# Eight orders of the high-part and low-part matmuls in layer 1 of a two-layer backbone

## The chip, the core and the metric

The kernel runs on one NeuronCore of a Trainium2 chip. The engines that matter here are TensorE (PE in the profile, with its weight loads as a row of their own, PEld), VectorE (DVE), ScalarE (ACT) and SyncE (SP), which issues the DMAs. The metric is the time of one execution on the device in microseconds. The kernel as it stands takes 1834.39 us, the median of three runs (1833.95 to 1835.42).

## The reference

Two layers act on 256 tokens of width 2048. Layer 0 (retention and Fourier mixing, with a context of 256 more tokens) is not touched by the table of orders. Layer 1 is the short gated convolution:

```python
def _odd_layer(h, w_in, conv_w, w_out, rows):
    bg, cg, xt, g = jnp.split(h @ w_in, 4, axis=-1)
    y = bg * _conv3(cg * xt, conv_w, rows) * jax.nn.silu(g)
    return y @ w_out
...
    x = x + gate_x * yx
...
return _rmsnorm(x, final_norm_w)
```

`h` is the modulated norm of `x` (256 by 2048), `w_in` is 2048 by 16384, `w_out` is 4096 by 2048. All of it is float32.

## The kernel before, in words

Every activation lies channel-major: channels on the 128 partitions, the 256 tokens on the free axis. A product in float32 is carried by three passes of a faster format: each operand is split exactly into a high and a low part of 12 bits (x = hi + lo), and hi·hi + lo·hi + hi·lo is summed in PSUM. An activation tile holds its two parts side by side, 512 columns: high in 0 to 255, low in 256 to 511.

The weights stream in as tiles of 128 by 2048 (1 MB, `load_raw`, issued by SP, three buffers). Each tile is cut into quarters of 512 columns (`split_w`): ScalarE casts a quarter to its high part `whi` (line 95), VectorE subtracts to get the low part `wlo` (line 59). There are six buffers of each, so ScalarE and VectorE work ahead of TensorE by up to six quarters, and then wait until a matmul frees one.

`group_t` (line 119) makes 256 output columns. It runs over weight tiles (`kt`), their quarters (`pc`), and in a quarter over four blocks of 128 by 128 weights: two k-chunks (`k2`) by two halves of the output columns (`m`). For each block there are two matmuls. The one with the high part of the weights streams all 512 columns of the activation (high and low part), so it makes hi·hi in the left half of a PSUM bank and hi·lo in the right half. The one with the low part of the weights streams only the 256 columns of the high activations into the left half. In what follows H is a matmul of the first kind (128x512 in the profile) and L one of the second kind (128x256). Each matmul has a weight load of its own, also where two in a row use the same weights. `lr` (line 178) later adds the two halves.

`group_t` serves layer 0 (for the keys with two streams at once, `hx` and `hc`), the output projection of layer 0 (`w0o`), layer 1 and its output projection (`w1o`). In layer 1 the loop over `b` (line 700) calls it four times for each of 16 blocks, 64 groups of two weight tiles in all: 64 x 2 x 4 x 4 = 2048 H and 2048 L, on the input tiles `h1_0` to `h1_7` (`h` in the profile). The output projection then runs over the tiles `y1` (`y`): seven blocks by `group_t` (448 H and 448 L) and the eighth by `group_d`, whose matmuls are all of 256 columns, three in a row for each block of weights: high by high, high by low, low by high. `group_n` (`gN`) is a form with 512 columns throughout.

A scheduler that simulates the program sets the order on each engine. It keeps the order in which `group_t` issues its matmuls, except where an operand would be late: there it pulls matmuls of the next group in between. At the start of layer 1, where the tiles `h1` are still being made (lines 196 to 198), the first two groups are interleaved in this way.

Of the kernel before, what the change touches and what calls it, by code (L numbers as in the profile page):

```python
"""Two-layer hybrid retention / Fourier / short-convolution backbone with a context prefix.

Everything runs in channel-major form (channels on partitions, tokens on the free axis), so
modulation, gates, norms' weights and the convolution are per-partition scalars, and no
activation is ever transposed.  Matrix products are carried by float32r passes: each operand is
split exactly into two 12-bit parts (x = hi + lo) and hi*hi + lo*hi + hi*lo is accumulated in PSUM.
"""
# [13 lines left out]
D = 2048  # L21
T = 256
H = 8
DK = 128
P = 128
EPS = 1e-6

# columns of the packed per-channel vectors
C_C, C_CC, C_AB0, C_NW0, C_ABG, C_NW1, C_FNW, C_LOG, C_CV, C_SEL = 0, 16, 32, 64, 80, 144, 160, 176, 192, 288
N_COLS = 290  # L30
# columns of the packed shape-only tables
# [4 lines left out]
def body(tc, a, out):  # L36
    nc = tc.nc
    es = ExitStack()
    with es:
# [27 lines left out]
        # ---------------------------------------------------------------- constants  # L67
# [11 lines left out]
        # ---------------------------------------------------------------- weight stream  # L79
# [5 lines left out]
        def split_w(raw, spare=None):  # L85
            """Exact 12-bit parts of a weight tile, by quarters; the last quarter can use spare slots."""
            parts = []
            for pc in range(4):
                sl = raw[:, pc * 512:(pc + 1) * 512]
                if spare and pc == 3:  # L90
                    hi, lo = spare()
                else:
                    hi = wp.tile([P, 512], F32R, tag="whi", bufs=6, name="whi")
                    lo = wp.tile([P, 512], F32R, tag="wlo", bufs=6, name="wlo")
                nc.scalar.copy(hi[:], sl)  # L95
                sub(lo[:], sl, hi[:])
                parts.append((hi, lo))
            return parts
# [6 lines left out]
        def bg():  # L105
            """One background task at every second weight tile."""
            if quiet[0]:
                return
            turn[0] ^= 1
            if tasks and turn[0]:  # L110
                tasks.pop(0)()
# [7 lines left out]
        def group_t(wd, i0, nkt, streams):  # L119
            """Channel-major product of 256 output columns; per stream a pair of banks [hi.W + lo.hi | lo.W]."""  # L120
            ps = [psum("gT") for _ in streams]
            for kt in range(nkt):
                raw = load_raw(wd[i0 + kt])
                bg()
                for pc, (hi, lo) in enumerate(split_w(raw)):
                    for k2 in range(2):
                        kc = kt * 8 + pc * 2 + k2
                        fst, lst = kc == 0, kc == nkt * 8 - 1
                        for t, st in zip(ps, streams):
                            x = st[kc // 2]  # L130
                            for m in range(2):
                                c0 = k2 * 256 + m * 128
                                mm(t[:, m, :], hi[:, c0:c0 + 128], x[:, kc % 2, :], fst, False)
                                mm(t[:, m, 0:256], lo[:, c0:c0 + 128], x[:, kc % 2, 0:256], False, lst)
                    if pc % 2:
                        hook()
            return ps

        def group_d(wd, i0, nkt, x):
            """As group_t for one stream, with all three products summed in place: a bank of two column halves."""  # L140
            t = bank("gD")
            for kt in range(nkt):
                raw = load_raw(wd[i0 + kt])
                bg()
                for pc, (hi, lo) in enumerate(split_w(raw)):
                    for k2 in range(2):
                        kc = kt * 8 + pc * 2 + k2
                        xh, xl = x[kc // 2][:, kc % 2, 0:256], x[kc // 2][:, kc % 2, 256:512]
                        for m in range(2):
                            c0 = k2 * 256 + m * 128  # L150
                            o = t[:, m * 256:m * 256 + 256]
                            mm(o, hi[:, c0:c0 + 128], xh, kc == 0 and m == 0, False)
                            mm(o, hi[:, c0:c0 + 128], xl, False, False)
                            mm(o, lo[:, c0:c0 + 128], xh, False, kc == nkt * 8 - 1)
            return t

        def group_n(wd, i0, streams):
            """Token-major product of 512 output columns; per stream a pair of banks (token tiles)."""
            ps = [psum("gN") for _ in streams]
            for kt in range(4):  # L160
                raw = load_raw(wd[i0 + kt])
                bg()
                for pc, (hi, lo) in enumerate(split_w(raw)):
                    kc = kt * 4 + pc
# [13 lines left out]
        def lr(pool, t, name="t2", bufs=5):  # L178
            """Sum of the two halves of a channel-major bank pair."""
# [6 lines left out]
        def rstd_bc(pool, ps_sum, n):  # L186
            """Reciprocal root of the mean plus eps, from sums already broadcast over partitions."""
# [5 lines left out]
        def modulate(pool, dst, x, col, shift, rs):  # L193
            """dst (hi | lo) = x * col * rs + shift."""
# [6 lines left out]
        def split_act(dst, y):  # L201
            """dst[:, m] = (hi | lo) of y[:, m]."""
# [9 lines left out]
        # ---------------------------------------------------------------- start: norms and first modulation  # L212
# [39 lines left out]
        # 1 + scale bias  # L252
# [14 lines left out]
        def gather():  # L267
            """Copies the four partial rows out of PSUM."""
# [4 lines left out]
        def modulation(e, gs):  # L273
            """Rows to columns; (scale, shift) of both streams, then the modulated chunks of this eighth."""
# [88 lines left out]
        # ---------------------------------------------------------------- background: remaining modulation rows  # L363
# [13 lines left out]
        # ---------------------------------------------------------------- retention  # L377
# [3 lines left out]
        # lg: [0:16] = -log gamma, [16:32] = 256 log gamma, [32:48] = log gamma; (forward, backward) x heads  # L381
# [17 lines left out]
        def rope(t, tag, cc, ss):  # L399
            """t [P, 2 heads, 256] (PSUM or SBUF); rotates halves of the partition axis."""  # L400
# [9 lines left out]
        def retention(hh, m, q, k, kc, v):  # L410
            """Stages of one head: scores, weighted values, norm; returns them with the place of the result."""
# [80 lines left out]
        # ---------------------------------------------------------------- Fourier mixing  # L492
        f_es = ExitStack()
        fp = f_es.enter_context(tc.tile_pool(name="fou", bufs=1))
        def table(src, n, name):
            """Splits a table of cosines and sines."""
# [8 lines left out]
        th, tl = table(a["dft"], 512, "t")            # tokens: cos | sin  # L505
        ch, cl = table(a["dftc"], 256, "c")           # channels: cos 0..127 | cos 128, -sin 1..127
        # folded tokens-by-channels operands: even part, odd part (column 0 stays zero), middle channel
# [11 lines left out]
        def fold(pu):  # L519
            """Even and odd parts of u over the channel index, tiles [P, (token half, group), channel]."""  # L520
# [19 lines left out]
        def fourier(g):  # L540
            """Stages of one channel group: the channel tables by its weights, the token transform, their product."""
            got = {}

            def mm3(o, x, y, start, stop):
                """o += x^T y, operands given as (hi, lo)."""
# [86 lines left out]
        # ---------------------------------------------------------------- output projection, layer 0  # L632
        # gv: gate0 | scale1 | shift1 | gate1
# [9 lines left out]
        def project(wd, xs, gcol, xin, acc, first=None, post=None):  # L643
            """x1 = xin + gate * projection; returns its rows' reciprocal root mean square, after which all
            blocks of x1 but the last are scaled by the columns from post on."""
# [5 lines left out]
            for b in range(8):  # L651
# [16 lines left out]
                else:  # L668
# [4 lines left out]
                    # the root's table is in place before it is needed  # L673
# [20 lines left out]
        # ---------------------------------------------------------------- layer 1  # L694
# [5 lines left out]
        y1 = []  # L700
        for b in range(16):
            tcg, = group_t(w1, b * 8, 2, [h1])
            scg = lr(l1, tcg, "scg", 2)
            txt, = group_t(w1, b * 8 + 2, 2, [h1])
# [12 lines left out]
            tbg, = group_t(w1, b * 8 + 4, 2, [h1])  # L717
            sbg = lr(l1, tbg)
            mul(cv[:], cv[:], sbg[:])
            tg, = group_t(w1, b * 8 + 6, 2, [h1])  # L720
# [20 lines left out]
def _tile_t(w):  # L741
    """[K, 256] -> [K/1024, 128, 2048]: channel-major weight tiles of 8 k-chunks by 256 columns."""
# [4 lines left out]
def _tile_n(w):  # L747
    """[2048, 512] -> [4, 128, 2048]: token-major weight tiles of 4 k-chunks by 512 columns."""
# [7 lines left out]
def _layout(i):  # L756
# [16 lines left out]
    # scale | shift columns of layer 0, an eighth (256 channels) at a time  # L773
    s = np.stack([ada[0][:, D:2 * D], ada[0][:, 0:D]])            # 2, k, n
    s = s.reshape(2, 4, 4, P, 8, 256).transpose(4, 1, 3, 2, 0, 5)  # e, kq, p, k4, sc/sh, n
# [23 lines left out]
    for b in range(16):  # L799
        for part in (1, 2, 0, 3):                                  # cg, xt, bg, g  # L800
# [4 lines left out]
    # tables of shapes alone  # L805
    j = np.arange(256).reshape(2, P)
    dd = (np.arange(256)[None, None, :] - j[:, :, None]).astype(np.float32)          # i - j
# [4 lines left out]
    cs, sn = np.cos(ang).T.astype(np.float32), np.sin(ang).T.astype(np.float32)      # 64, T  # L812
# [27 lines left out]
```

## Time and profile before

| what | value |
|---|---|
| time, median of 3 runs | 1834.39 us |
| profiled execution: span from the first to the last instruction | 1833.4 us |
| TensorE busy with matmuls | 98 % of the span |
| weight loads (they overlap the matmuls) | 84 % |
| VectorE, ScalarE | 66 %, 49 % |
| layer 1, first H to first matmul of `y` | 930.0 to 1641.9 us |
| output projection of layer 1, `group_t` part | 1641.9 to 1797.2 us |
| mean granted clock of TensorE | 0.995 |

The profiled execution took 1833.4 us between its first and last instruction, 1.0 us less than the median of the timed runs. The page gives the end of a matmul as a modelled value: a matmul of 512 columns is listed with 391 ns, though the next one starts 230 ns later. What a matmul costs in a full stream is therefore read from start to start, in the timeline, or from a window with its count of matmuls.

### The profile page before, as it was taken

What the parts mean: (1) busy time and instruction counts of PE and PEld (TensorE: products, weight loads), DVE (VectorE), ACT (ScalarE), POOL (GpSimd) and SP (SyncE); (2) the same over time, 40 slices, a digit from 0 to 9 for tenths busy, and PEclk for the clock granted to TensorE, in tenths of its full rate; (3) what the DMA queues carried; (4) which work ended last, traced back from release to release, by engine and by line L of the source; (5) the groups of instructions that cost most, each with busy time, mean ns of one, the idle gap of its engine ahead of it and who ended that gap; (6) DMA issues with size and microseconds to landing.
All of it is one profiled execution on the core that took longest, in us unless ns stands there. A gap on an engine that the chain in (4) does not pass through costs nothing.

```text
span 1833.4 us, 26739 instructions
## 1 busy us (share of the span) xinstructions
PE 1792.8 (98%) x10200; PEld 1541.9 (84%) x10200; DVE 1202.4 (66%) x1862; ACT 906.0 (49%) x1491; POOL 0.2 (0%) x4
## 2 busy tenths in 40 slices
PE   5999999999999999999999999999999999999997
PEld 3667888888888888888978888888888888888887
DVE  5347747557477777777587888666666666665554
ACT  4225626345265554444555555555555555555553
POOL 0000000000000000000000000000000000000000
PEclk8999999999999999999999999999999999999999
DMA  9886445545466676777547877555555555555552
GB/s 389 327 319 246 144 156 184 180 165 186 150 238 250 243 258 229 262 291 287 196 161 253 299 279 288 191 187 197 191 184 191 196 188 185 189 199 186 186 192 105
DMA packets 58449, 400.87 MB, mean 219 GB/s; under 512 B 6480, under 2 KB 6608, under 8 KB 11088
## 3 DMA queue, kind: packets, MB, share of 16 engines
q1 hardware_dynamic: 58320, 399.16, 60.5%
q8 instruction: 80, 1.31, 0.3%
q14 instruction: 49, 0.40, 0.1%
HBM read 397.03 MB, written 2.10 MB: 218 GB/s over the span
## 4 chain that ended last, share of the span: by engine, by line
PE 95%; DVE 2%; ACT 1%; DMA 1%; issue 0%; SPq 0%; DVEq 0%
PE gT L56 70%; PE gN L56 12%; PE gD L56 3%; PE gemv L56 2%; PE pk L56 1%; PE o L56 1%; PE pvc L56 1%; PE pvx L56 1%; PE pP L56 1%; PE S L56 1%; PE pz L56 1%; PE py L56 1%; DMA raw<-w0s 1%; PE pq L56 1%; DMA xT<-xT 0%
## 5 line engine op out<-in xcount | busy, mean ns | idle before, releaser
L95 ACT CAST whi<-raw 128x512 fp32r<-128x512 f32 x1088 | 670.9, 622 | 746.1 <-PE gT L56 535.8
L59 DVE TENSOR_TENSOR wlo<-raw,whi 128x512 fp32r<-128x512 f32 x1088 | 738.3, 690 | 452.4 <-ACT whi L95 436.7
L56 PE MATMUL gT<-h,whi 128*128 128x512 f32 x2048 | 711.3, 392 | 4.2 <-DVE h L198 4.2
L56 PE MATMUL gT<-h,wlo 128*128 128x256 f32 x2048 | 573.2, 280 | 0.0
L56 PEld LDWEIGHTS gT<-h,whi 128*128 128x128 f32 x2048 | 383.6, 187 | 88.8 <-issue 4.5
L56 PEld LDWEIGHTS gT<-h,wlo 128*128 128x128 f32 x2048 | 387.5, 189 | 0.7 <-DVE wlo L59 0.3
L56 PE MATMUL gT<-hx,whi 128*128 128x512 f32 x704 | 254.5, 401 | 1.6 <-ACT v L478 1.6
L56 PE MATMUL gT<-hx,wlo 128*128 128x256 f32 x704 | 197.9, 281 | 0.1
L371 DVE CUSTOM_DVE_ANT_0 raw<-raw,scb 128x2048 f32<-128x2048 f32 x64 | 146.5, 2290 | 48.0 <-DMA raw<-adaT 45.0
L56 PEld LDWEIGHTS gT<-hx,whi 128*128 128x128 f32 x704 | 132.2, 188 | 32.3 <-ACT v L478 2.1
L56 PE MATMUL gT<-y,whi 128*128 128x512 f32 x448 | 155.3, 391 | 0.0
L56 PE MATMUL gN<-whi,hx 128*128 128x512 f32 x448 | 139.3, 392 | 0.0
L56 PEld LDWEIGHTS gT<-hx,wlo 128*128 128x128 f32 x704 | 132.9, 189 | 1.8 <-DVE wlo L59 0.7
L56 PE MATMUL gT<-y,wlo 128*128 128x256 f32 x448 | 125.4, 280 | 0.0
L56 PEld LDWEIGHTS gT<-y,whi 128*128 128x128 f32 x448 | 83.8, 187 | 18.4
L56 PEld LDWEIGHTS gN<-whi,hx 128*128 128x128 f32 x448 | 83.5, 188 | 16.9
L56 PE MATMUL gN<-wlo,hx 128*128 128x512 f32 x224 | 87.3, 390 | 0.0
L56 PEld LDWEIGHTS gT<-y,wlo 128*128 128x128 f32 x448 | 84.7, 189 | 0.0
L56 PE MATMUL gT<-yB,whi 128*128 128x512 f32 x224 | 79.5, 399 | 0.0
L56 PE MATMUL gT<-yA,whi 128*128 128x512 f32 x224 | 79.4, 398 | 0.0
L56 PE MATMUL gT<-yB,wlo 128*128 128x256 f32 x224 | 62.9, 281 | 0.0
L56 PE MATMUL gT<-yA,wlo 128*128 128x256 f32 x224 | 62.9, 281 | 0.0
(233 smaller groups left out, 1792.4 us busy)
## 6 DMA issues: line engine op xcount, KB each, us to landing
raw<-w SPq DMA_DIRECT2D x200, 1024.0 KB, 4.9
raw<-adaT SPq DMA_DIRECT2D x64, 1024.0 KB, 4.9
raw<-ada SPq DMA_DIRECT2D x32, 1024.0 KB, 6.9
raw<-w0o SPq DMA_DIRECT2D x32, 1024.0 KB, 4.9
raw<-w1o SPq DMA_DIRECT2D x32, 1024.0 KB, 4.8
raw<-w0s SPq DMA_DIRECT2D x8, 1024.0 KB, 5.7
xT<-xT SPq DMA_DIRECT2D x4, 512.0 KB, 6.7
cT<-ctxT SPq DMA_DIRECT2D x4, 512.0 KB, 16.2
```

What stands on the lines that cost most here:

```text
L56: nc.tensor.matmul(o, l, r, start=start, stop=stop, skip_group_check=True)
L59: nc.vector.tensor_tensor(o, x, hi.bitcast(F32), op=ALU.subtract)
L95: nc.scalar.copy(hi[:], sl)
L371: nc.vector.tensor_tensor_reduce(out=raw[:], in0=raw[:], in1=scb[:], scale=1.0, scalar=0.0, op0=ALU.mult, op1=ALU.add, accum_out=gv[:, j:j ...
```

## The change

`group_t` gets the name of an order, and a table gives for each name the order of the matmuls in a quarter. The four blocks of a quarter are numbered 0 to 3 (0 and 2 go to the first bank, 1 and 3 to the second). Beside H and L there are A and B, the left and right 256 columns of H as two matmuls with the same weights. The first quarter of each group keeps the old order, since it clears PSUM. The 64 groups of layer 1 take the eight names in turn, so each order comes eight times. All sums stay the same; only the order in which they are added changes.

```diff
-        def group_t(wd, i0, nkt, streams):
+        ORDERS = {
+            "pairs": "H0 L0 H1 L1 H2 L2 H3 L3",
+            "twos": "H0 H1 L0 L1 H2 H3 L2 L3",
+            "fours": "H0 H1 H2 H3 L0 L1 L2 L3",
+            "mirrored": "H0 L0 L1 H1 H2 L2 L3 H3",
+            "low first": "L0 H0 L1 H1 L2 H2 L3 H3",
+            "one split": "A0 B0 L0 H1 L1 H2 L2 H3 L3",
+            "two split": "A0 B0 L0 A1 B1 L1 H2 L2 H3 L3",
+            "last split": "H0 L0 H1 L1 H2 L2 A3 B3 L3",
+        }
+
+        def group_t(wd, i0, nkt, streams, order="pairs"):
+
             ps = [psum("gT") for _ in streams]
+            last = nkt * 8 - 1
             for kt in range(nkt):
                 raw = load_raw(wd[i0 + kt])
                 bg()
                 for pc, (hi, lo) in enumerate(split_w(raw)):
-                    for k2 in range(2):
-                        kc = kt * 8 + pc * 2 + k2
-                        fst, lst = kc == 0, kc == nkt * 8 - 1
+
+                    todo = ORDERS["pairs" if kt + pc == 0 else order].split()
+                    for n, (what, j) in enumerate((x[0], int(x[1])) for x in todo):
+                        k2, m = j // 2, j % 2
+                        kc, c0 = kt * 8 + pc * 2 + k2, j * 128
+                        stop = kc == last and not any(x[1] == str(j) for x in todo[n + 1:])
+                        w = (lo if what == "L" else hi)[:, c0:c0 + 128]
+                        a0, a1 = {"H": (0, 512), "A": (0, 256), "B": (256, 512), "L": (0, 256)}[what]
                         for t, st in zip(ps, streams):
-                            x = st[kc // 2]
-                            for m in range(2):
-                                c0 = k2 * 256 + m * 128
-                                mm(t[:, m, :], hi[:, c0:c0 + 128], x[:, kc % 2, :], fst, False)
-                                mm(t[:, m, 0:256], lo[:, c0:c0 + 128], x[:, kc % 2, 0:256], False, lst)
+                            mm(t[:, m, a0:a1], w, st[kc // 2][:, kc % 2, a0:a1], kc == 0 and what == "H", stop)
...
+        names = list(ORDERS)
         for b in range(16):
-            tcg, = group_t(w1, b * 8, 2, [h1])
+            o4 = [names[(4 * b + i + b // 2) % 8] for i in range(4)]
+            tcg, = group_t(w1, b * 8, 2, [h1], o4[0])
...
-            txt, = group_t(w1, b * 8 + 2, 2, [h1])
+            txt, = group_t(w1, b * 8 + 2, 2, [h1], o4[1])
...
-            tbg, = group_t(w1, b * 8 + 4, 2, [h1])
+            tbg, = group_t(w1, b * 8 + 4, 2, [h1], o4[2])
...
-            tg, = group_t(w1, b * 8 + 6, 2, [h1])
+            tg, = group_t(w1, b * 8 + 6, 2, [h1], o4[3])
```

The loop over streams now lies inside the loop over the matmuls of a quarter. So the three key groups of layer 0, which have two streams, change their order too, though they keep the name "pairs": each matmul is now issued for `hx` and then for `hc`.

How the instructions stand on TensorE is shown at three places. A row is the output tile, the two operands and the moving shape; "x2" is two in a row. First, the third group of layer 1 ("fours") where it goes over into the fourth ("mirrored"), as it stands after the change:

```order
L56 MATMUL gT<-h_7_8141,whi 128x512 x4
L56 MATMUL gT<-h_7_8141,wlo 128x256 x4
L56 MATMUL gT<-h_0_8134,whi 128x512
L56 MATMUL gT<-h_0_8134,wlo 128x256
...
L56 MATMUL gT<-h_1_8135,whi 128x512
L56 MATMUL gT<-h_1_8135,wlo 128x256 x2
L56 MATMUL gT<-h_1_8135,whi 128x512 x2
L56 MATMUL gT<-h_1_8135,wlo 128x256 x2
L56 MATMUL gT<-h_1_8135,whi 128x512
```

Before, every quarter of layer 1 was four times one `whi` and one `wlo` row; now there are runs of one, two and four of a kind, and the quarter of `h_0` between the two groups is in the old order.

Second, the seam between the last group of layer 1 ("two split", operand `h_7`) and the first group of the output projection (operand `y_0`). Before:

```order
L56 MATMUL gT<-h_6_8140,wlo 128x256
L56 MATMUL gT<-h_7_8141,whi 128x512
L56 MATMUL gT<-h_7_8141,wlo 128x256
...
L56 MATMUL gT<-y_0_8638,whi 128x512
L56 MATMUL gT<-y_0_8638,wlo 128x256
```

And now:

```order
L56 MATMUL gT<-h_6_8140,wlo 128x256
L56 MATMUL gT<-h_7_8141,whi 128x256 x2
L56 MATMUL gT<-h_7_8141,wlo 128x256
L56 MATMUL gT<-h_7_8141,whi 128x256 x2
L56 MATMUL gT<-h_7_8141,wlo 128x256
L56 MATMUL gT<-h_7_8141,whi 128x512
L56 MATMUL gT<-h_7_8141,wlo 128x256
...
L56 MATMUL gT<-y_0_8638,whi 128x512
```

The two matmuls of 512 columns at the front of the quarter have become four of 256. The output projection itself stands as before.

Third, the key groups of layer 0, as a piece of the difference (a minus is the old place, a plus the new one):

```order
 L56 MATMUL gT<-hx_82,whi 128x512
-L56 MATMUL gT<-hx_82,wlo 128x256
-L56 MATMUL gT<-hx_82,whi 128x512
-L56 MATMUL gT<-hx_82,wlo 128x256
 L56 MATMUL gT<-hc_90,whi 128x512
+L56 MATMUL gT<-hx_82,wlo 128x256
 L56 MATMUL gT<-hc_90,wlo 128x256
+L56 MATMUL gT<-hx_82,whi 128x512
 L56 MATMUL gT<-hc_90,whi 128x512
+L56 MATMUL gT<-hx_82,wlo 128x256
 L56 MATMUL gT<-hc_90,wlo 128x256
```

What stood as four matmuls of one stream and then four of the other now goes from stream to stream with each matmul, so that two of a kind stand side by side.

## The prediction

> **What bounds the kernel now.** I read the page first, then the waits inside layer 1, then the stream of matmuls from start to start. From the page, the parts on busy time, on the chain that ended last and on the costliest groups:
>
> ```profile
> PE 1792.8 (98%) x10200; PEld 1541.9 (84%) x10200; DVE 1202.4 (66%) x1862; ACT 906.0 (49%) x1491; POOL 0.2 (0%) x4
> ...
> PE gT L56 70%; PE gN L56 12%; PE gD L56 3%; PE gemv L56 2%; PE pk L56 1%; PE o L56 1%; PE pvc L56 1%; PE pvx L56 1%; PE pP L56 1%; PE S L56 1%; PE pz L56 1%; PE py L56 1%; DMA raw<-w0s 1%; PE pq L56 1%; DMA xT<-xT 0%
> ...
> L56 PE MATMUL gT<-h,whi 128*128 128x512 f32 x2048 | 711.3, 392 | 4.2 <-DVE h L198 4.2
> L56 PE MATMUL gT<-h,wlo 128*128 128x256 f32 x2048 | 573.2, 280 | 0.0
> ...
> L56 PE MATMUL gT<-y,whi 128*128 128x512 f32 x448 | 155.3, 391 | 0.0
> ...
> L56 PE MATMUL gT<-yB,whi 128*128 128x512 f32 x224 | 79.5, 399 | 0.0
> L56 PE MATMUL gT<-yA,whi 128*128 128x512 f32 x224 | 79.4, 398 | 0.0
> ```
>
> TensorE is the bound: 70% of the chain that ended last is `gT`. In the 2048 pairs of layer 1 (`h`) it sat idle for 4.2 us in all, before the first matmul. The waits between 947 and 1640 us (waiting line, its releaser, us in total, times, longest) say the same from the other side:
>
> ```profile
> ACT whi L95 <- PE gT L56: 302.4, 450, 2.3
> DVE wlo L59 <- ACT whi L95: 188.2, 285, 1.6
> ACT whi L95 <- DVE wlo L59: 23.8, 32, 0.8
> ```
>
> No row has PE as the one that waits. ScalarE waits for TensorE to free a buffer, so the weight parts lie ready. What counts is only how closely matmuls follow one another. The windows (us, busy with counts by engine, clock, DMA) of layer 1, of its output projection and of that of layer 0 hold only pairs H, L:
>
> ```profile
> 1000.00:1640.00 640.00, 640.00 (x3694) 564.29 (x3693) 444.45 (x698) 331.76 (x548) 0.00 (x0) 1.00 0.61 214
> 1643.00:1796.00 153.00, 153.00 (x884) 134.90 (x883) 89.22 (x137) 80.87 (x138) 0.00 (x0) 1.00 0.55 191
> 755.00:899.00 144.00, 144.00 (x817) 124.78 (x817) 101.66 (x148) 69.92 (x114) 0.00 (x0) 1.00 0.74 271
> ```
>
> Two of each count reach in from before the window. A pair costs 640 / 1846 = 346.7 ns in layer 1, 153 / 441 = 346.9 ns in its projection, but 144 / 407.5 = 353.4 ns in the projection of layer 0: same shapes, same order, same clock (1.00), no idle time, 6.7 ns more. The page's groups show it too: a `whi` matmul is listed with 391 or 392 ns in the quick stretches and with 398 or 399 in the slow one. So the stream H L H L can run in two gears, and layer 1 is now in the quicker one from end to end. This, more than the 224 added matmuls, decides what the change does.
>
> **What a run of one kind costs.** Matmuls of 256 columns in a row, the eighth block of the projection (128 with the high part, 64 with the low part; timeline: start, us, instruction, xcount):
>
> ```profile
> L56 PE MATMUL gD<-y,whi 128*128 128x256 f32 x128 | 23.1, 283 | 0.0
> ```
>
> ```profile
> 1797.17 0.40 PE L56 MATMUL gD<-y,whi 128*128 128x256 f32 x2
> ...
> 1820.20 1.02 PE L56 MATMUL tot<-acc,ones 128*128 128x256 f32 x4
> ```
>
> 23.03 us / 192 = 120.0 ns. There, too, two in a row use the same weights, and that saves nothing visible. Matmuls of 512 columns in a row, going over into H L H L:
>
> ```profile
> 545.60 0.39 PE L56 MATMUL gN<-wlo,hx 128*128 128x512 f32 x1
> 545.82 0.62 PE L56 MATMUL gN<-whi,hx 128*128 128x512 f32 x2
> 546.28 0.39 PE L56 MATMUL gN<-wlo,hx 128*128 128x512 f32 x1
> 546.50 0.39 PE L56 MATMUL gT<-hx,whi 128*128 128x512 f32 x1
> 546.73 0.28 PE L56 MATMUL gT<-hx,wlo 128*128 128x256 f32 x1
> 546.84 0.40 PE L56 MATMUL gT<-hx,whi 128*128 128x512 f32 x1
> 547.08 0.28 PE L56 MATMUL gT<-hx,wlo 128*128 128x256 f32 x1
> 547.19 0.40 PE L56 MATMUL gT<-hx,whi 128*128 128x512 f32 x1
> 547.43 0.28 PE L56 MATMUL gT<-hx,wlo 128*128 128x256 f32 x1
> 547.55 0.40 PE L56 MATMUL gT<-hx,whi 128*128 128x512 f32 x1
> ```
>
> 545.60 to 546.28 is 0.68 us for three: 226.7 ns each. 120.0 + 226.7 = 346.7 ns, exactly the quick pair. So 120.0 and 226.7 are the floor of a matmul, reached by runs of one kind and by the quick gear; the slow gear is the floor plus 6.7 ns for each change from H to L and back. And the rows show how the slow gear is entered: out of a run of 512s, 546.84 to 547.55 is already 0.71 us for two pairs, or 355 ns a pair with rows that are rounded to 10 ns.
>
> **The change part by part.**
>
> *Splits.* Where A and B take the place of H, 2 x 120.0 stand for 226.7: +13.3 ns. The three orders with splits have 1 + 2 + 1 = 4 in a quarter, each order comes in 8 groups with 7 changed quarters: 224 splits, 224 x 13.3 = +3.0 us. On the path, since nothing but TensorE's stream sets the time.
>
> [...]
>
> *Order in layer 1.* In runs a quarter of "pairs" goes four times from H to L and back, "twos" 2, "fours" 1, "mirrored" 2, "low first" 4, "one split" 3, "two split" 2 (A, B and L are of one size, so its first six make one run), "last split" 3: 21 in all. 56 x 21 = 1176, and the 64 first quarters in the old order have 4 each: 1432 in place of 2048. At the floor all that costs 0; in the slow gear throughout 1432 x 6.7 = +9.6 us. A gain is left out: no window lies under the floor. The nearest row in between is the start of layer 1, where the scheduler interleaves two groups and so makes runs of two:
>
> ```profile
> 939.00 0.40 PE L56 MATMUL gT<-h,whi 128*128 128x512 f32 x1
> 939.25 0.28 PE L56 MATMUL gT<-h,wlo 128*128 128x256 f32 x1
> 939.37 0.62 PE L56 MATMUL gT<-h,whi 128*128 128x512 f32 x2
> 939.83 0.28 PE L56 MATMUL gT<-h,wlo 128*128 128x256 f32 x1
> 939.94 0.40 PE L56 MATMUL gT<-h,whi 128*128 128x512 f32 x1
> 940.17 0.40 PE L56 MATMUL gT<-h,wlo 128*128 128x256 f32 x2
> ...
> 945.68 0.64 PE L56 MATMUL gT<-h,whi 128*128 128x512 f32 x2
> ...
> 946.62 0.39 PE L56 MATMUL gT<-h,whi 128*128 128x512 f32 x1
> ```
>
> From 939.00 to 946.62 there are 22 H and 21 L in 19 changes. The floor would be 22 x 226.7 + 21 x 120.0 = 7507 ns; it took 7.62 us, 110 more: 5.8 ns a change. I take this one: the stretch has runs of two and single pairs, as the new orders have, on the same tiles. 1432 x 5.8 = +8.3 us.
>
> *The projection of layer 1* is not edited, but it follows the last group of layer 1 without a gap, and its 448 pairs now inherit a quick stream. The new last group ends in runs of 256s and two pairs. Bounds: 0, or 448 x 6.7 = +3.0 us. As a gear can change inside it, I take half, +1.5 us.
>
> *Key groups of layer 0.* Three groups of 64 pairs, 192 in all, some now as runs of two. Bounds are -192 x 6.7 = -1.3 us and +1.3 us; they stand in both gears now, so 0.
>
> *Feed.* The matmuls of a quarter need their weight parts up to 227 ns sooner ("low first") or later ("fours"). The waits above leave room: ScalarE is held by TensorE 450 times, up to 2.3 us. The first groups are tighter. There the seventh block of `h1` is taken 7 matmuls (some 1.2 us) sooner. Before, VectorE wrote it from 942.52 to 943.40, and TensorE took it with the second matmul of the row at 945.68:
>
> ```profile
> 942.52 0.88 DVE L198 SCALAR_TENSOR_TENSOR h<-modt,mods,h 128x256 fp32r<-128x256 f32 x2
> ```
>
> Some 2.5 us of room, of which 1.2 go: 0. If the cover were gone, it would cost those 1.2 us once.
>
> *Sum.* 3.0 + 8.3 + 1.5 = 12.8 us on a span of 1833.4 gives 1846.2; the profiled span lies 1.0 us below the median of the runs, so the time is **1847 us**, +0.7%.
>
> **The rivals.**
>
> *The order is free* (not slower). The quick gear survives, or each order settles at the floor; then only the splits are left: 1834.4 + 3.0 = 1837.4, which is +0.16% and inside the 0.2% (3.7 us) that a measurement can tell from no change. For it: layer 1 and its projection stay in the quick gear for 850 us, through all group seams, and it is entered right after the mixed stretch, at 946.62. Against it: the mixed stretch itself, and the rows at 546.84. It decides if the quick gear comes back within a quarter after each run. [...]
>
> *Every change costs, to the end.* Layer 1 at 6.7 ns a change (9.6 us), the projection in the slow gear throughout (3.0), splits 3.0: 15.6 us, 1850.0.
>
> *The low part is late.* In "low first" TensorE meets the part that VectorE makes last. If each of its 56 quarters waited for the 227 ns by which it comes sooner, 12.7 us more, about 1850 with the splits. Against it: the 302.4 us in which ScalarE waits for TensorE.
>
> *A gain.* If the reordered keys turned the later parts of layer 0 quick, the projection there (448 pairs) would gain 3.0 us and layer 1 might stay at the floor: about 1834; faster than the 0.2% only if more of layer 0 follows. The gear there is set anew at each run of `gN`, so hardly.
>
> **How the numbers follow.** The forecast, most changes above the floor, 0.60 (about 1841 to 1849); the order is free, 0.25 (1835 to 1838); every change costs, 0.10; the low part is late, 0.03; a gain, 0.02. The likeliest case alone is 1841 to 1849; with the free order and the full price inside, the range is 1836.8 to 1850.5. Slower: 0.60 + 0.10 + 0.03, less a little for a sum that ends just inside the bound, 0.72; same: 0.25; faster: 0.03.
>
> **What would show it.** Right, if the mean of `gT<-h,whi` rises from 392 towards 396 to 399 where it is still 512 columns, `y,whi` from 391, a window over layer 1 shows the changed stream some 11 us longer with no row of PE waiting, and "fours" groups cost least. Splits: 120 ns from start to start in A, B, L. Wrong, if the windows of `h` and `y` still give 346.7 ns for a pair and only the 3.0 us appear, or if PE shows up among those that wait.

## The result, and the profile after

The changed kernel takes 1846.10 us (median of three runs, 1844.91 to 1846.92) against 1834.39: ratio 1.0063, interval 1.0043 to 1.0083. It is slower by 11.7 us; 1847 us had been predicted. Of the 39 runs of the old kernel on record, two that took 4123.18 and 6331.16 us are compared with nothing here; two others took 1849.71 and 1851.01 us, and are taken up below.

From the profile's page for the changed kernel: the span, the busy times, and the groups that answer to those shown before.

```profile
span 1844.3 us, 27092 instructions
...
PE 1803.6 (98%) x10424; PEld 1553.7 (84%) x10424; DVE 1201.2 (65%) x1862; ACT 903.3 (49%) x1491; POOL 0.2 (0%) x4
...
L56 PE MATMUL gT<-h,whi 128*128 128x512 f32 (+1 forms) x2272 | 688.0, 375 | 4.2 <-DVE h L213 4.2
L56 PE MATMUL gT<-h,wlo 128*128 128x256 f32 x2048 | 508.4, 280 | 0.0
...
L56 PE MATMUL gT<-y,whi 128*128 128x512 f32 x448 | 158.3, 399 | 0.0
...
L56 PE MATMUL gT<-yB,whi 128*128 128x512 f32 x224 | 79.5, 399 | 0.0
L56 PE MATMUL gT<-yA,whi 128*128 128x512 f32 x224 | 79.4, 398 | 0.0
```

The 375 ns of `h,whi` mixes two shapes. The view that keeps shapes apart gives for it:

```profile
L56 PE MATMUL gT<-h,whi 128*128 128x512 f32 x1824 | 615.6, 397 | 4.2 <-DVE h L213 4.2
...
L56 PE MATMUL gT<-h,whi 128*128 128x256 f32 x448 | 87.5, 282 | 0.0
```

1824 + 448 is 2048 and the 224 splits. The listed mean of the H that are left went from 392 to 397 ns, and that of the `y,whi` of the projection, whose code was not edited, from 391 to 399. TensorE still waits for nothing inside layer 1, after the 4.2 us at its first matmul. The list of waits from 945 to 1648 us starts with the same two rows as before, and again no row has PE as the one that waits:

```profile
ACT whi L95 <- PE gT L56: 316.0, 445, 1.4
DVE wlo L59 <- ACT whi L95: 199.5, 302, 1.4
```

The windows of layer 1, of its projection and of the projection of layer 0:

```profile
1000.00:1640.00 640.00, 640.00 (x3839) 566.47 (x3838) 435.76 (x685) 324.97 (x541) 0.00 (x0) 1.00 0.59 209
1652.00:1806.00 154.00, 154.00 (x874) 133.47 (x873) 88.02 (x135) 79.74 (x135) 0.00 (x0) 1.00 0.53 186
753.00:896.00 143.00, 143.00 (x812) 124.06 (x811) 100.19 (x147) 69.04 (x114) 0.00 (x0) 1.00 0.74 271
```

154 us / 436 pairs = 353.2 ns: the projection of layer 1 has changed from the quick gear (346.7 ns a pair) to the slow one, in which the projection of layer 0 stays (143 / 405 = 353.1 ns). Where the time went is told by four starts in the timeline: that of the first scores of layer 0, and the first matmul of layer 1, of its projection, and of the eighth block.

```profile
167.63 1.02 PE L56 MATMUL S<-q,k 128*128 128x256 f32 x4
...
927.57 0.48 PE L56 MATMUL gT<-h,whi 128*128 128x512 f32 x1 [4.15 <-DVE h L213]
...
1649.78 0.40 PE L56 MATMUL gT<-y,whi 128*128 128x512 f32 x1
...
1808.07 0.40 PE L56 MATMUL gD<-y,whi 128*128 128x256 f32 x2
```

Layer 1 takes 722.2 us for 711.8 (+10.4), the projection 158.3 for 155.3 (+3.0); layer 1 begins 2.5 us earlier, of which 1.4 us lie before the first scores, where nothing was changed. Together that is +10.9 us, the difference of the spans.

Every matmul of the 64 groups can be priced in the trace, from its start to the next start, less the floor of 226.7 or 120.0 ns. The groups of an order nearly always cost the same (the first group of layer 1, with its start, is left out). A change is one from H to L and back, counted as in the prediction:

| order | over the floor per group | changes per group | per change |
|---|---|---|---|
| pairs | 218 ns | 32 | 6.8 ns |
| last split | 162 | 25 | 6.5 |
| one split | 155 | 25 | 6.2 |
| fours | 141 | 11 | 12.8 |
| two split | 104 | 18 | 5.8 |
| twos | 69 | 18 | 3.8 |
| mirrored | 53 | 18 | 2.9 |
| low first | 32 in six of eight | 32 | 1.0 |

"Pairs", the old order, is now the dearest. The code of those groups is what it was; they cost 0 before. Quarter by quarter, these groups run at the price of the slow gear (22 to 34 ns a quarter). Five of the other orders settle at a steady price of their own, from 6 ns a quarter ("twos", "mirrored") to 20 ("one split", "last split"), "fours" goes up and down between 13 and 19, and "low first" comes back to the floor from its third quarter on, in those six groups.

### The profile page after: what moved, and what is told of

It is laid out like the page before. It is cut to its first block, busy times and chain, and to the rows that moved or that the text cites. A ratio compares the mean times of both kernels' runs of the same rounds, so it can differ in the third digit from the quotient of the medians.

```text
span 1844.3 us, 27092 instructions
## 1 busy us (share of the span) xinstructions
PE 1803.6 (98%) x10424; PEld 1553.7 (84%) x10424; DVE 1201.2 (65%) x1862; ACT 903.3 (49%) x1491; POOL 0.2 (0%) x4
## 4 chain that ended last, share of the span: by engine, by line
PE 97%; DVE 1%; ACT 1%; DMA 0%; issue 0%; SPq 0%; DVEq 0%
PE gT L56 72%; PE gN L56 12%; PE gD L56 2%; PE gemv L56 2%; PE o L56 1%; PE pvx L56 1%; PE pk L56 1%; PE pvc L56 1%; PE pP L56 1%; PE S L56 1%; PE pq L56 1%; PE pz L56 1%; PE py L56 1%; DMA xT<-xT 0%; DVE nacc L65 0%; DVE modt L211 0%
## 5 line engine op out<-in xcount | busy, mean ns | idle before, releaser
L56 PE MATMUL gT<-h,whi 128*128 128x512 f32 (+1 forms) x2272 | 688.0, 375 | 4.2 <-DVE h L213 4.2
L56 PE MATMUL gT<-h,wlo 128*128 128x256 f32 x2048 | 508.4, 280 | 0.0
L56 PEld LDWEIGHTS gT<-h,whi 128*128 128x128 f32 x2272 | 392.2, 189 | 62.0 <-issue 4.5
L56 PEld LDWEIGHTS gT<-h,wlo 128*128 128x128 f32 x2048 | 379.5, 189 | 25.5
L56 PE MATMUL gT<-y,whi 128*128 128x512 f32 x448 | 158.3, 399 | 0.0
L196 ACT COPY lr_r<-gT 128x512 f32<-128x512 f32 x103 | 60.1, 583 | 10.6 <-PE gT L56 10.5
```

The lines of the kernel that those rows point to most:

```text
L56: nc.tensor.matmul(o, l, r, start=start, stop=stop, skip_group_check=True)
L196: nc.scalar.copy(r[:], t[:, :, 256:512])
```

## Experiments

The theory: the stream of matmuls has a state (perhaps a phase between the weight loads and the matmuls). A stream H L H L keeps its gear until something upsets it, and an upset anywhere can set the gear for all that follows. The rival: an order has a price where it stands, and nowhere else.

Three kernels below were run ten times or more (one group, and back, the last version). The others were run once each, so for them the profile of that run, and the place in it at which the gear changes, carries more than the time.

### One group of 64

```diff
+        def o1(k):
+            return "last split" if k == 8 else None
...
-            tcg, = group_t(w1, b * 8, 2, [h1])
+            tcg, = group_t(w1, b * 8, 2, [h1], o1(4 * b + 0))
```

> The kernel before, with the ninth of the 64 groups of layer 1 alone in the order "last split" (7 splits); everything else, the loop over streams too, as before. Theory (two gears, kept until something upsets them): the runs of 256 columns in that one group put the stream into the slow gear, and the 55 groups behind it and the output projection, though unedited, stay there: (55 x 32 + 448) pairs x 6.7 ns = 14.8 us, and 0.1 us for the splits, so +14.9 us on 1834.4. A pair after the group takes 353.4 ns, before it 346.7. Rival (a change of order costs where it stands and no further): 7 splits x 13.3 ns plus 25 changes x 6.7 ns, 0.3 us, no difference that can be measured.

Measured: 1849.52 us (ten runs, 1847.70 to 1850.92) against 1834.87, ratio 1.0074 (1.0054 to 1.0094), +14.7 us. Windows before the group, after it, and in the projection:

```profile
1000.00:1019.00 19.00, 19.00 (x111) 16.63 (x110) 15.70 (x26) 8.47 (x14) 0.00 (x0) 1.00 0.83 295
1031.00:1640.00 609.00, 609.00 (x3449) 528.14 (x3448) 410.43 (x645) 307.95 (x512) 0.00 (x0) 1.00 0.58 205
1655.00:1810.00 155.00, 155.00 (x879) 134.37 (x878) 88.52 (x135) 80.05 (x136) 0.00 (x0) 1.00 0.52 184
```

19 us / 54.5 pairs is 349 ns (one matmul more or less in so short a window is 3 ns; pair by pair the starts give 346.7), then 609 / 1723.5 = 353.4 and 155 / 438.5 = 353.5 ns. Reordering one group of 64 (28 of the 2048 pairs) costs more than reordering 56 of them. The rival falls: the loss lies in code that was not edited.

### And back

The same kernel, and two groups later one quarter in the order H0 L0 H1 H2 L1 H3 L2 L3.

```diff
+            "nudge": "H0 L0 H1 H2 L1 H3 L2 L3"}
...
-            return "last split" if k == 8 else None
+            return {8: "last split", 10: {1: "nudge"}}.get(k)
```

> The kernel with one group of layer 1 in the order "last split" (the ninth), which took 14.7 us more than before, and in the eleventh group one quarter as H0 L0 H1 H2 L1 H3 L2 L3, where the H1 is one of 241 ns in the profile of that kernel. Theory: the quick gear is set again there and kept to the end of the projection; layer 1 costs 0.5 us more than before, its projection 155.3 us, time 1835. Rival (the slow gear has another cause that began with the ninth group, for instance late weight parts or a shifted feed): 1849.5 us as without the quarter.

Measured: 1834.50 us (ten runs, 1833.71 to 1835.93), ratio 0.9995 (0.9977 to 1.0013). The windows between the two places, after the second, and in the projection:

```profile
1031.00:1041.00 10.00, 10.00 (x59) 8.68 (x58) 6.35 (x9) 4.24 (x8) 0.00 (x0) 1.00 0.69 228
1050.00:1635.00 585.00, 585.00 (x3377) 511.42 (x3376) 398.92 (x632) 302.62 (x501) 0.00 (x0) 1.00 0.59 206
1643.00:1794.00 151.00, 151.00 (x873) 132.00 (x872) 87.49 (x135) 79.63 (x135) 0.00 (x0) 1.00 0.55 190
```

Between the two places the stream is slow: the first window is short, but from start to start the 32 pairs of the tenth group take 353.5 ns each. Behind the second place a pair takes 585 / 1687.5 = 346.7 ns, and in the projection 151 / 435.5 = 346.7 ns. The order of a few matmuls in one quarter takes away what the order of one group had brought. Late weights or a shifted feed, had the reordered group brought them, would still be there; that rival gave 1849.5 us.

### The nudge where the stream was slow before

This is the kernel before, with that order (the nudge) in the eighth quarter of the first group of the projection of layer 0, or, in a second kernel, one quarter later:

```diff
-        t_out, = group_t(a["w0o"], 0, 4, [ys])
+        t_out, = group_t(a["w0o"], 0, 4, [ys], {7: "nudge"})
```

> The kernel before with one quarter changed in the whole program: the eighth quarter of the first group of the output projection of layer 0, H0 L0 H1 H2 L1 H3 L2 L3. In the slow gear of the kernel before, the H of that stretch follow one another with 232, 241 and 236 ns in turn to the next matmul, and the H1 of this quarter is one of 241. In the mixed stretch at the start of layer 1 two H side by side led from a slow stretch into a quick one where the first of them was one of 241 ns (945.68 us), and two L side by side behind that did not end it. Theory (the gear is a phase that the order of a few matmuls can set): the 418 pairs behind the quarter go to 346.7 ns, the projection of layer 0 takes 2.8 us less (156.8 for 159.6 us). Rival (the slow gear belongs to this stage, by its operands, or to runs of two): 159.6 us as before or up to 0.01 us more.

> As the kernel with the one changed quarter, but one quarter later, where the H1 is one of 236 ns. Theory of the phase: in the mixed stretch two H side by side that began with one of 235 or 236 ns left the stream slow, so the projection of layer 0 stays slow, 159.6 us. Rival (two H and two L side by side quicken the stream wherever they stand): 156.8 us.

The window from 755 to 893 us, first of the one, then of the other:

```profile
755.00:893.00 138.00, 138.00 (x799) 120.69 (x798) 99.86 (x145) 67.92 (x112) 0.00 (x0) 1.00 0.76 278
```

```profile
755.00:893.00 138.00, 138.00 (x783) 119.61 (x782) 98.56 (x143) 67.39 (x110) 0.00 (x0) 1.00 0.75 272
```

138 / 398.5 = 346.3 ns against 138 / 390.5 = 353.4 ns. From its first matmul to the first of the eighth block the projection takes 156.84 us with the first nudge and 159.59 with the second (159.62 before). The first kernel takes 1831.73 us against 1834.17, one run. So runs of two do not quicken a stream wherever they stand. In the slow gear the next matmul starts 232, 241 and 236 ns after an H, in turn. Where the two H side by side began with one of 241 ns, the stream turned quick (here, in the kernel "and back", and at 945.68 us of the kernel before); where they began with one of 236 ns, it did not. A pair that begins with one of 232 ns was not tried.

The second kernel took 1850.93 us, +16.8, which neither theory had expected of it. Its profile shows where that lies. In layer 1 a background transfer (`adaT`) came late and held VectorE up, and two low parts were late for TensorE, the first by 0.61 us (waits from 1004 to 1024 us, and the timeline of TensorE at the first):

```profile
DVE raw L377 <- DMA raw<-adaT: 5.0, 2, 2.7
...
PE gT L56 <- DVE wlo L59: 0.9, 2, 0.6
```

```profile
1008.24 0.39 PE L56 MATMUL gT<-h,whi 128*128 128x512 f32 x1
1009.24 0.39 PE L56 MATMUL gT<-h,wlo 128*128 128x256 f32 x1 [0.61 <-DVE wlo L59]
1009.46 0.39 PE L56 MATMUL gT<-h,whi 128*128 128x512 f32 x1
```

Until 1005 us the stream was quick (45 us / 129.5 pairs = 347.5 ns), from 1012 on it is slow (628 / 1776 = 353.6 ns, the second wait included):

```profile
960.00:1005.00 45.00, 45.00 (x261) 39.34 (x260) 31.82 (x47) 23.87 (x40) 0.00 (x0) 1.00 0.69 249
1012.00:1640.00 628.00, 627.74 (x3554) 544.12 (x3554) 425.94 (x668) 317.93 (x529) 0.00 (x0) 1.00 0.59 208
```

The edit of this kernel ends in layer 0, and two of the 39 runs of the unedited kernel took 1849.71 and 1851.01 us, some 15 us above the others. No profile of these two was kept; that they ran into the same upset fits their size and is not shown. Nor does every upset change the gear: in the kernel before, one L at 998.62 us was followed after 168 ns in place of 117, and the pairs behind it stay at 346.7 ns.

### A stall on purpose

So a stall can change the gear too. To bring one about, one weight tile of layer 1 was loaded two, three or four times in a row into its buffer; all matmuls stay in the old order.

```diff
-            nc.sync.dma_start(raw[:], src)
+            for _ in range(again[0]):
+                nc.sync.dma_start(raw[:], src)
+            again[0] = 1
...
+            again[0] = 2 if b == 2 else 1
```

> The kernel before, its matmuls in the old order throughout, but one weight tile of layer 1 (the first of the ninth group, at about 1019 us) is loaded twice in a row into the same buffer, so it lands some 5 us later. Weight parts lie 5.7 us ahead of their matmul there, and a tile more in the raw buffers: theory: no stall of TensorE, no change of gear, time as before. Theory of gears if TensorE does stall: any stall sets the gear anew, and behind it a pair takes 346.7 or 353.4 ns from there to the end of the projection, 0 or up to 14.7 us.

> The same tile loaded three times in a row, landing some 10 us late. Theory: TensorE stalls once, by a few us at most; the gear behind the stall is then set by the moment at which the stream starts again: +the stall alone (0 to 4 us) if it starts in the quick gear, +14 us more if in the slow one. Rival (a gear is changed only by runs of matmuls of one size, not by a stall): the stall alone, pairs at 346.7 ns behind it.

> The same tile loaded four times in a row, landing some 15 us late, so a longer stall (4 to 9 us) and another moment of starting again. Theory and rival as for three loads: the stall alone, or the stall and 14 us more by the slow gear; the two kernels need not end in the same gear.

Measured: 1849.45, 1858.63 and 1848.86 us (before, beside them: 1833.25), one run each. With two loads TensorE did stall, against the expectation, though only for 0.21 and 0.10 us:

```profile
1053.30 0.39 PE L56 MATMUL gT<-h,whi 128*128 128x512 f32 x1
1053.74 0.39 PE L56 MATMUL gT<-h,wlo 128*128 128x256 f32 x1
1053.96 0.39 PE L56 MATMUL gT<-h,whi 128*128 128x512 f32 x1
```

The next L starts 0.44 us after the 1053.30, where 0.23 is usual, and the H behind it 0.22 us later instead of 0.12. With those 0.3 us, layer 1 and its projection take 14.5 us more than before. The stall stands some 33 us behind the start of the group with the tile loaded twice, and it came as in the nudge one quarter later, by a late `adaT` and VectorE (waits from 1000 to 1060 us):

```profile
DVE raw L380 <- DMA raw<-adaT: 5.0, 4, 2.0
...
PEld gT L56 <- DVE wlo L59: 0.4, 1, 0.4
```

Whether the second load made `adaT` late is not shown. That the pairs are slow from this stall on is. With three loads the stall is 6.7 us, with four 11.7 us, at the first matmuls of the tile itself:

```profile
1026.11 0.79 PE L56 MATMUL gT<-h,whi 128*128 128x512 f32 x1 [6.74 <-ACT whi L99]
```

```profile
1032.01 0.80 PE L56 MATMUL gT<-h,whi 128*128 128x512 f32 x1 [11.65 <-ACT whi L99]
```

Yet the longer stall gave the shorter time. The windows behind the stall, for two, three and four loads:

```profile
1060.00:1640.00 580.00, 580.00 (x3285) 502.92 (x3284) 386.74 (x609) 293.41 (x487) 0.00 (x0) 1.00 0.57 202
```

```profile
1040.00:1640.00 600.00, 600.00 (x3398) 520.32 (x3397) 401.90 (x629) 303.31 (x504) 0.00 (x0) 1.00 0.57 204
```

```profile
1043.00:1640.00 597.00, 597.00 (x3445) 522.08 (x3445) 408.34 (x643) 309.15 (x511) 0.00 (x0) 1.00 0.58 209
```

580 / 1641.5 = 353.3, 600 / 1698 = 353.4 and 597 / 1721.5 = 346.8 ns a pair. A stall costs itself and then 0 or 14 us, by the gear in which the stream goes on. Behind the two long ones the granted clock is 0.50 for another 6.4 and 4.9 us, with an H every 640 ns (427 and 213), and the gear is there as soon as it is back at 1.00. Whether the stall or the return of the clock set it, these runs do not tell.

### Splits alone, one order alone, the loop alone

```diff
+            "all split": "A0 B0 L0 A1 B1 L1 A2 B2 L2 A3 B3 L3"}
...
+            return "all split"
```

> The kernel before, with every H of layer 1 outside the first quarters split into A and B (1792 splits), so that a quarter is a run of twelve matmuls of 256 columns. Theory: a run of one size is at the floor, 120.0 ns each, so the splits cost 1792 x 13.3 ns = 23.9 us; the first quarters of the 64 groups, four pairs each, stand between runs and are slow, 256 x 6.7 ns = 1.7 us; the output projection is entered from a run and is slow, 3.0 us: +28.6 us. Rival (the order is free, only matmuls count): +23.9 us, with the projection at 346.7 ns a pair. Rival (the second load of the same weights is saved): clearly under 23.9 us.

Here all 64 groups of layer 1 have this order. Measured: 1863.36 us (one run), +28.5 against 1834.87. Layer 1 takes 736.7 us (+24.9, of which 23.9 are the sum worked out for the splits; the first quarters take 0.9 over the floor), the projection 158.3 (+3.0). The second load of the same weights is not saved.

```diff
+            "low first": "L0 H0 L1 H1 L2 H2 L3 H3"}
...
+            return "low first"
```

> The kernel before, with all 64 groups of layer 1 in the order "low first": the same number of H and L and of changes between them as in "pairs", but two L side by side behind the first quarter of each group and two H side by side at each seam of groups. Theory of two gears: the gear is set anew at each such place; in the changed kernel a group of this order cost 32 ns over the floor in six cases of eight, so 64 x 32 ns = 2.0 us if it always lands so, and up to 64 x 218 ns = 14 us if it falls into the slow gear; the output projection 0 or 3.0 us after that. Rival (the number of changes between H and L sets the price): as many changes as in the quick kernel before, so 0.

Measured: 1844.14 us (one run), layer 1 +7.2 us, projection +3.0. Four groups in a row, each 64 matmuls in the same order:

```profile
1031.21:1042.33 11.12, 11.12 (x65) 9.72 (x64) 8.19 (x12) 5.45 (x9) 0.00 (x0) 1.00 0.76 281
1042.33:1053.63 11.30, 11.30 (x66) 9.80 (x64) 10.52 (x19) 5.46 (x9) 0.00 (x0) 1.00 0.73 275
1053.63:1064.75 11.12, 11.12 (x65) 9.73 (x64) 8.66 (x13) 5.45 (x9) 0.00 (x0) 1.00 0.79 287
1064.75:1076.05 11.30, 11.30 (x66) 9.81 (x64) 9.26 (x14) 6.51 (x11) 0.00 (x0) 1.00 0.75 276
```

From the sixth group on they cost 32 and 202 ns over the floor in turn, start to start: each group seems to hand the other gear to the next. The number of changes between H and L does not set the price, and the 2.0 us that had been expected were an extrapolation from eight groups of which seven stood behind "mirrored".

The loop over streams, moved inside:

```diff
-                    for k2 in range(2):
...
+                    for n, (what, j) in enumerate((x[0], int(x[1])) for x in todo):
...
                         for t, st in zip(ps, streams):
-                            x = st[kc // 2]
-                            for m in range(2):
```

> The kernel before with the loop over streams inside the loop over the matmuls of a quarter, and no other order anywhere: the second part of the change alone. In the changed kernel the three key groups of layer 0 took 1.0 us less from start to end than before. Theory: that comes from this loop, by runs of two and fewer changes; expected -1.0 us between the first S and the last ss, layer 1 and its projection at 346.7 ns a pair. Rival: the key groups gained by chance at their feed; expected 0.

Measured: 1833.41 us (one run). The first scores and the last sum of squares of the retention (`ss`), first in the kernel before, then with the loop changed:

```profile
169.06 1.02 PE L56 MATMUL S<-q,k 128*128 128x256 f32 x4
...
524.28 0.59 PE L56 MATMUL ss<-sq,ones 128*128 128x256 f32 x2
```

```profile
168.06 1.02 PE L56 MATMUL S<-q,k 128*128 128x256 f32 x4
...
522.11 0.59 PE L56 MATMUL ss<-sq,ones 128*128 128x256 f32 x2
```

That is 355.2 us and 354.1 us: -1.2 us, from the second part of the change alone. Layer 1 (711.8) and its projection (155.3) are as before.

### A version that is faster than both

The nudge in the projection of layer 0 and the new loop over streams, with layer 1 in the old order:

```diff
+                    for n, (what, j) in enumerate((x[0], int(x[1])) for x in todo):
...
                         for t, st in zip(ps, streams):
...
+        t_out, = group_t(a["w0o"], 0, 4, [ys], {7: "nudge"})
```

> The one changed quarter together with the loop over streams inside the loop over the matmuls (keys of layer 0), layer 1 in the old order: a candidate that is faster than both kernels. Theory: -2.8 us in the projection of layer 0 and -1.0 to -1.2 us in the keys, 1830.4 us against 1834.4, ratio 0.998. Rival: the slow gear comes back at the next upset, -1 to -2 us, not to be told from no change.

Measured: 1831.74 us (eleven runs, 1829.30 to 1833.63) against 1834.17, ratio 0.9985 (0.9976 to 0.9994). In its profile the projection of layer 0 takes 156.8 us, the stretch of the keys 1.1 us less than before, layer 1 and its projection stay quick (635 us / 1832 pairs = 346.6 ns, 150 / 433 = 346.4):

```profile
1000.00:1635.00 635.00, 635.00 (x3666) 559.89 (x3664) 439.03 (x688) 329.16 (x544) 0.00 (x0) 1.00 0.61 212
1640.00:1790.00 150.00, 150.00 (x868) 132.25 (x867) 86.91 (x134) 79.02 (x134) 0.00 (x0) 1.00 0.55 190
```

1830.4 us had been expected. In this profile the gain of the keys is lost again before the projection: at 719 us TensorE waits 0.7 us for a low part, and the stretch from the last `ss` to the projection takes 217.65 us in place of 216.41. The kernel with the nudge alone took as long (1831.73 us, one run), so what the new loop adds to it is not shown. The gain of the two together is small but clear of zero.

## Why the prediction was right, and where it was not

*What bounds the kernel* held: TensorE's stream, with no wait on it. *That there are two gears*, read from three windows with the same shapes and clock, was the step that carried the forecast; one changed group, and one nudge back, showed that an edit can set the gear of unedited code.

*Splits*, +3.0 us: right. With every H of layer 1 outside the first quarters split, layer 1 took 24.9 us more, with 23.9 worked out from the same 13.3 ns. The Trainium skill ("TensorE: Matmul & The Clock Gate", section "Back-to-back issue gap") gives N / 2.4 + 2.5 ns at full clock for a single matmul of N columns, and says itself that a stream of weight loads and matmuls goes otherwise. An estimate by that formula is 2.5 ns a split, 4.5 us for 1792; the measured 24.9 us decide.

*Order in layer 1*, +8.3 us: it measured 10.4 less the 3.0 of the splits, +7.4. The sum was near by luck; the way to it failed. It took one price, 5.8 ns, for each change from H to L and back. There is no such price: it goes from 1.0 ns ("low first") to 12.8 ("fours") in the table above, and one and the same order costs 32 or 202 ns a group. "Fours" was to cost least and is the fourth dearest of eight. The stretch from which the 5.8 ns were read ran its single pairs in the slow gear (944.62 to 945.68 us: three pairs, 353.3 ns each), so they were mostly the price of a gear, and not of a change. In the changed kernel the groups in the old order pay it; the others have the prices named there.

*The projection of layer 1*, +1.5 us: it measured the upper bound, +3.0. Half was taken because a gear might change inside; it did not, and TensorE was not upset there in this profile.

*Key groups*, 0: they gained 1.0 us, inside the bounds of 1.3. In layer 1 the prediction counted that runs of two leave fewer changes; for the keys, where some of the stream was taken to be slow, it did not count this.

*Feed*, 0: right. *The sum* of 12.8 us on the span measured 10.9: 3.0 + 7.4 + 3.0 - 1.0 for the terms, and -1.4 before the first scores, which nothing in the change touches; that first start lies between 166.3 and 169.1 us in the profiles here. That the total came so near is luck in part: the terms were off by -0.9, +1.5 and -1.0 us, which nearly cancel.

*The rivals.* "The order is free" fell with the projection, 353.2 ns a pair with unedited code. "Every change costs, to the end" describes the projection, not layer 1 (7.4 us for its 9.6). "The low part is late" has no row among the waits. "A gain" did not come: the projection of layer 0 stayed at 353.1 ns a pair, and only the keys themselves gained 1.0 us.

## What to carry to other kernels

Where one engine's stream is the bound, price the same shapes in several windows before pricing an edit. Here a difference of 2% between them, at one clock and with no wait, was the sign that the stream has a state; then an edit can cost or gain far from where it stands. Such a state is cheap to test: make one small change of order early in a long stretch, and read the window behind it. A single run can meet an upset of its own, so look in its profile for the place at which the pace changes.

## What the runs showed of the hardware

A stream of alternating matmuls of 512 and 256 columns, each with its own weight load, ran at 346.7 or 353.4 ns a pair, for hundreds of microseconds, at the same granted clock (1.00) and with no wait. The long runs of one size were at the floor (192 matmuls of 256 columns at 120.0 ns; three of 512 columns at 226.7). With a stall of 0.3 us came 14.5 us of loss in this way, and a stall of 11.7 us cost less than one of 6.7. In two kernels that differ only in where two H stand side by side in a slow stretch, it turned quick in the one (346.3 ns) and not in the other (353.4). Behind stalls of 6.7 and 11.7 us the granted clock was 0.50 for some microseconds, and an H took 427 ns in place of 227. What the state is made of, no run here shows.
